# Three edits to the gates of a two-layer decoder kernel: where the decay rates are exponentiated, how the skips are loaded, and how the gates' weights lie

## The chip, the cores and the metric

The kernel runs on one core of a Trainium2 chip. The time is the device time of one execution in microseconds (us). A profile of one further execution is at hand: for every engine, the start and length of each instruction, and what each engine waited for. The engines are PE (TensorE, matrix products), DVE (VectorE), ACT (ScalarE), POOL (GpSimd) and SP (SyncE, which only issues transfers). "PEld" are the weight loads of PE, which run beside its matmuls.

## The reference, cut to what matters

The program is a decoder trunk of two layers on 512 tokens of width 1024. Each layer is a half-step SwiGLU feed-forward, a mixer, and a second half-step feed-forward. Layer 0's mixer is a Mamba-2 head group beside an mLSTM head group; layer 1's is a sparse attention. The change touches the gates of layer 0's mixer and the small parameters that go with them:

```python
z, xbc, dt_raw, qm, km, vm, om, ig, fg = split_cols(h @ w_in, HY_SPLITS)   # dt_raw: 16 columns, ig: 4, fg: 4
dt = softplus(dt_raw + dt_bias)          # (512, 16)
A  = -exp(a_log)                         # the decay rates, 16 numbers
y  = ssd_chunked(xs, dt, A, B, C, 128)
y  = y + xs * d_skip[:, None]            # the skips, 16 numbers, one for each head of 64 channels
hm = mlstm_chunked(qm, km, vm, ig + igate_bias, fg + fgate_bias, 128)
```

Everything is float32. The kernel holds a float32 matrix as two parts, a high part that the matmul's reduced format holds exactly and the low rest, and forms a product from three matmuls: high by high, high by low, low by high.

## The kernel before, in words

The kernel runs six stages in turn: `ffn00`, `mix0` (layer 0's mixer), `ffn01`, `ffn10`, `mix1` and `ffn11`. It keeps the activations in SBUF, channels on partitions, and streams the weights: SP loads a block of a weight matrix into one of four buffers (`raw`), ACT and DVE split it into its two parts in one of five buffers (`form`: ACT copies the high part, L240 or L501, and DVE subtracts it from the raw block, L243 or L503), and PE multiplies.

**The feed-forward stages** take the 2816 hidden columns 256 at a time, in eleven units. From the third unit on, a unit's products are seven half-size products in the manner of Strassen (`seven`, from L626): their weights are sums and differences of four raw blocks (DVE, L496), they accumulate in PSUM pairs `pA`, `pB` and `pD`, and ACT copies some intermediate sums out of PSUM (`keep`, L651) before PE may go on adding to the same pair. Some blocks are split in another way: ACT writes the negated high part (L534), a transfer issued by POOL adds the raw block to it (L535), and ACT writes the high part (L536). One unit is 168 matmuls. The order of the instructions in these stages is set by a planner in the kernel (`Plan`), which gives each step a cost and a due time and issues the steps in the order of its own plan; `plan.tail` holds the last instruction planned for each engine.

**The stage `mix0`** is written out in program order, and a scheduler of the compiler, which works on modelled times, orders it. It may also move instructions of `mix0` ahead into `ffn00` where they depend on nothing there. `hybrid` first weaves `gates` (from L1095) with `conv` (from L1018). `gates` loads the 24 gate columns of the input projection for the eight blocks of 128 channels (L1100 to L1102), loads the small parameters (L1104 to L1110), exponentiates and negates the decay rates (L1112, L1113), splits the gate weights (L1114), and multiplies: 24 matmuls of 24 weight columns by 512 tokens into `pgate` (L1117). The statement `issue_after(self.loads[AMID].ins)` (L1105) holds the small loads behind the 31st weight load of `ffn00`. Then `settle` sums the squares of the activations (`pssq`, L417), raises the mean to the power -1/2 on POOL (L430), and spreads the result over the partitions (`prow`, L438, and ACT, L465); every product of the stage is scaled by it (`rrow`). The gates are scaled (L1121), turned so that tokens lie on partitions (`pgt`, L1124), given their biases (L1133), and taken through a chain of small DVE steps to the decays of both head groups (L1134 to L1204). `conv` is six pairs of projections (`pxbc`), each 24 matmuls of 128 columns by 512 tokens, scaled (`u`, L1028), convolved (L1030 on POOL, L1033 on DVE) and activated (L1037).

The small parameters lie in one 128-column row of the constants, `consts[:, 7]`. Columns 72 to 119 hold the biases (24), the decay rates (16) and the skips (8 for each half of the partitions). Columns 32 to 63 hold the rotary frequencies of layer 1, written by 32 memsets on POOL (L1415).

Of the kernel before, what the change touches and what calls it, by code (L numbers as in the profile page):

```python
# [10 lines left out]
F32 = mybir.dt.float32  # L11
F32R = mybir.dt.float32r
AF = mybir.ActivationFunctionType
ALU = mybir.AluOpType
AX = mybir.AxisListType

P = 128
T = 512
NB = T // P
D = 1024  # L20
KC = D // P
# [193 lines left out]
class Trunk:  # L215
# [879 lines left out]
    def gates(self, w, cols, g):  # L1095


        nc = self.nc
        a = self.a
        raw = self.ring("raw")[1][:, 0 : KC * 24].rearrange("p (n w) -> p n w", w=24)  # L1100
        for o, c, n in cols:
            nc.sync.dma_start(raw[:, :, o : o + n], w[:, c : c + n].rearrange("(k p) n -> p k n", p=P))  # L1102

        vec = self.consts[:, 7, 72:120]  # L1104
        with self.tc.issue_after(self.loads[AMID].ins):  # L1105
            for o, n, name in ((0, 16, "hy_dt_bias"), (16, 4, "hy_fgate_bias"), (20, 4, "hy_igate_bias"), (24, 16, "hy_a_log")):
                nc.sync.dma_start(vec[:, o : o + n], a[name].partition_broadcast(P))
            ds = a["hy_d_skip"].rearrange("e (c two) -> two (e c)", two=2)
            for h in range(2):
                nc.sync.dma_start(vec[h * 64 : (h + 1) * 64, 40:48], ds[h].partition_broadcast(64))  # L1110
        gbias, nega, self.dskip = vec[:, 0:24], vec[:, 24:40], vec[:, 40:48]
        nc.scalar.activation(nega, nega, AF.Exp)  # L1112
        nc.vector.tensor_scalar(nega, nega, -1.0, None, op0=ALU.mult)  # L1113
        f = self.form(raw)  # L1114
        ps = self.mmps("pgate")
        for k in range(KC):
            self.mm3(ps[0:24], (f[0][:, k], f[1][:, k]), (self.xg[0][k], self.xg[1][k]), k == 0, k == KC - 1)  # L1117
        self.settle()
        yield
        t = self.tmp.tile([24, T], F32, name="gt", tag="t1")  # L1120
        nc.vector.tensor_tensor(t, ps[0:24], self.rrow[0:24], op=ALU.mult)  # L1121
        pt = self.aux("pgt", (NB, P))
        for b in range(NB):
            nc.tensor.transpose(pt[:, b, 0:24], t[:, b * P : (b + 1) * P], self.ident[0:24, 0:24])  # L1124
        box, used = self.box, [0]

        def st(name, n):
            used[0] += NB * n
            return box[:, used[0] - NB * n : used[0]].rearrange("p (b n) -> p b n", b=NB)

        tt, ts, stt = nc.vector.tensor_tensor, nc.vector.tensor_scalar, nc.vector.scalar_tensor_tensor
        x = st("gx", 24)
        tt(x, pt[:, :, 0:24], gbias.unsqueeze(1).to_broadcast([P, NB, 24]), op=ALU.add)  # L1133
        ts(x[:, :, 16:20], x[:, :, 16:20], -1.0, None, op0=ALU.mult)  # L1134


# [1 line left out]
        u, s, z, p = st("gu", 20), st("gs", 20), st("gz", 20), st("gp", 20)  # L1138
# [762 lines left out]
```

## Time and profile before

| | us |
|---|---|
| median of 3 runs | 2011.41 |
| lowest, highest | 2008.55, 2012.13 |
| the profiled execution's own time | 2005.02 |
| its span, first to last instruction | 2003.3 |
| PE busy | 1963.0 (98% of the span) |
| DVE busy | 1589.9 (79%) |
| ACT busy | 1172.9 (59%) |
| POOL busy | 272.7 (14%) |
| mean granted TensorE clock | 0.996 of full speed |

In the rows of the profile, "L501" is line 501 of the kernel; "form<-raw" is what an instruction writes and reads, buffer numbers left out. A row of a timeline has the start and the length in us, engine, line, operation, tiles and shapes, how many, and in brackets how long the engine sat idle before it and what ended that. Matmuls overlap, so a matmul's length is more than the distance to the next one. A row of the table of windows has the stretch, its length, the busy time of PE, PEld, DVE, ACT and POOL with the number of instructions, the granted TensorE clock, the mean busy share of the 16 DMA engines and GB/s. A row of transfers ends with the median time from issue to landing. `ACT_TABLE_LOAD` is ACT's change from one set of functions to another; "SPq" is SP's queue of transfers.

### The profile page before, as it was taken

To read this page: it belongs to the slowest core of one execution; us is meant where nothing else is said; L and a number is where in the kernel's file an instruction comes from. 1 tells how busy PE (TensorE), PEld (TensorE's weight loads), DVE (VectorE), ACT (ScalarE), POOL (GpSimd) and SP (SyncE) were. 2 spreads that over 40 slices of the span, in tenths; PEclk is the share of its full clock that TensorE was granted. 3 is DMA by queue.
4 is the path that set the end of the run, shared out by engine and by line. 5 is a ranking of instruction groups with operands and counts; after the bars stand their busy time and mean duration, and the time that the engine had idled before them with its cause. 6 is when DMAs were issued, how large, how long until landed. Compare 5 with 4: busy or idle time off the path is not lost. (4 is left out here: it accounts for less than half of the span.)

```text
span 2003.3 us, 34305 instructions
## 1 busy us (share of the span) xinstructions
PE 1963.0 (98%) x13828; PEld 1782.7 (89%) x13828; DVE 1589.9 (79%) x2348; ACT 1172.9 (59%) x1718; POOL 272.7 (14%) x335
## 2 busy tenths in 40 slices
PE   8999999999999999999999999999999999999998
PEld 6999999787788888999998899999966577999998
DVE  7988878886547648988888998978779948989886
ACT  6756657442345434757566566756668644757564
POOL 1000101321101011001002000101214421101010
PEclk9999999999999999999999999999999999999999
DMA  8565666433331232666665356665754202666564
GB/s 221 138 168 139 148 168 148 129 106 116 103 98 62 77 97 71 165 152 166 154 163 140 103 148 167 159 161 143 181 136 105 64 5 80 155 162 169 147 171 114
DMA packets 214438, 265.47 MB, mean 133 GB/s; under 512 B 14140, under 2 KB 187400, under 8 KB 214280
## 3 DMA queue, kind: packets, MB, share of 16 engines
q1 hardware_dynamic: 193632, 190.87, 32.1%
q0 software_dynamic: 20448, 72.36, 19.4%
q8 instruction: 108, 1.77, 0.4%
q14 instruction: 50, 0.41, 0.1%
q10 hardware_dynamic: 200, 0.06, 0.0%
HBM read 188.77 MB, written 2.14 MB: 95 GB/s over the span
## 5 line engine op out<-in xcount | busy, mean ns | idle before, releaser
L503 DVE TENSOR_TENSOR form<-raw,form 128x1024 fp32r<-128x1024 f32 (+1 forms) x327 | 387.2, 1188 | 106.2 <-ACT form L501 104.5
L501 ACT ACTIVATE form<-raw 128x1024 fp32r<-128x1024 f32 (+1 forms) x327 | 335.2, 1028 | 195.5 <-DVE raw L496 134.7
L281 PE MATMUL pA<-xf,form 128*128 128x256 f32 x1152 | 322.3, 280 | 2.5 <-ACT ft L651 2.4
L283 PE MATMUL pA<-xf,form 128*128 128x256 f32 x1152 | 321.9, 279 | 0.0
L282 PE MATMUL pA<-xf,form 128*128 128x256 f32 x1152 | 321.8, 279 | 0.0
L496 DVE TENSOR_TENSOR raw<-raw 128x1024 f32<-128x1024 f32 (+2 forms) x241 | 283.6, 1180 | 20.8 <-DMA raw<-in_ffn_w_up 9.5
L535 POOL DMA_DIRECT2D form<-raw x136 | 116.9, 860 | 1193.4 <-ACT form L534 1139.0
L281 PEld LDWEIGHTS pA<-xf,form 128*128 128x128 f32 x1152 | 216.9, 188 | 3.1 <-ACT ft L651 2.6
L282 PEld LDWEIGHTS pA<-xf,form 128*128 128x128 f32 x1152 | 216.8, 188 | 0.2
L283 PEld LDWEIGHTS pA<-xf,form 128*128 128x128 f32 x1152 | 216.9, 188 | 0.0
L534 ACT ACTIVATE form<-raw 128x1024 fp32r<-128x1024 f32 (+1 forms) x136 | 140.2, 1032 | 130.0 <-PE pD L283 68.4
L282 PE MATMUL pA<-hid,form 128*128 128x256 f32 x704 | 198.3, 282 | 2.8 <-DVE hid L503 2.8
L281 PE MATMUL pA<-hid,form 128*128 128x256 f32 x704 | 198.9, 283 | 0.5 <-ACT hid L501 0.5
L283 PE MATMUL pA<-hid,form 128*128 128x256 f32 x704 | 197.4, 280 | 0.0
L281 PE MATMUL pD<-xf,form 128*128 128x256 f32 x576 | 160.6, 279 | 0.0
L282 PE MATMUL pD<-xf,form 128*128 128x256 f32 x576 | 160.6, 279 | 0.0
L283 PE MATMUL pD<-xf,form 128*128 128x256 f32 x576 | 160.5, 279 | 0.0
L496 DVE TENSOR_TENSOR ft<-ft 128x256 f32<-128x256 f32 (+2 forms) x288 | 146.9, 539 | 4.4 <-ACT ft L754 0.4
L536 ACT ACTIVATE form<-raw 128x1024 fp32r<-128x1024 f32 (+1 forms) x136 | 139.0, 1023 | 0.0
L282 PEld LDWEIGHTS pA<-hid,form 128*128 128x128 f32 x704 | 132.3, 188 | 4.4 <-DVE hid L503 4.2
L281 PEld LDWEIGHTS pA<-hid,form 128*128 128x128 f32 x704 | 132.5, 188 | 1.4 <-ACT hid L501 0.9
L283 PEld LDWEIGHTS pA<-hid,form 128*128 128x128 f32 x704 | 132.4, 188 | 0.0
(450 smaller groups left out, 5168.0 us busy)
## 6 DMA issues: line engine op xcount, KB each, us to landing
form<-raw POOLq DMA_DIRECT2D x120, 512.0 KB, 5.9
raw<-in_ffn_w_gate SPq DMA_DIRECT2D x88, 512.0 KB, 4.6
raw<-in_ffn_w_up SPq DMA_DIRECT2D x88, 512.0 KB, 4.0
raw<-in_ffn_w_down SPq DMA_DIRECT2D x64, 512.0 KB, 4.9
raw<-in_hy_w_in SPq DMA_DIRECT2D x44, 512.0 KB, 3.8
raw<-in_ffn_w_down SPq DMA_DIRECT2D x32, 384.0 KB, 3.8
raw<-in_hy_w_out SPq DMA_DIRECT2D x16, 512.0 KB, 3.5
form<-raw POOLq DMA_DIRECT2D x16, 384.0 KB, 4.3
```

The lines of the kernel that those rows point to most:

```text
L281: mm(out, l[0], r[0], start=start, stop=False)
L282: mm(out, l[0], r[1], start=False, stop=False)
L283: mm(out, l[1], r[0], start=False, stop=stop)
L496: (self.p if pool else self.v)(n, lambda: e.tensor_tensor(out(), x(), y(), op=op), reads, writes)
L501: self.s(n, lambda: self.highs.append(nc.scalar.activation(hi(), src(), AF.Copy)), srck, hik)
L503: n, lambda: nc.vector.tensor_tensor(lo(), src(), hi().bitcast(F32), op=ALU.subtract), srck + hik, lok
L534: self.s(n, lambda: nc.scalar.activation(f()[:, 1], raw, AF.Copy, scale=-1.0), rawk, lok)
L535: self.plan.add("gpsimd", 0.85, lambda: nc.gpsimd.dma_start(f()[:, 1], raw, accum_op=ALU.add), rawk + lok, lok, 5.5)
L536: self.s(n, lambda: nc.scalar.activation(f()[:, 0], raw, AF.Copy), rawk, hik)
```

## The change

Three edits in `gates`. The exponential and the negation of the decay rates, and the spreading of the skips, are held behind the last planned instruction of ACT and of DVE. The skips are loaded by one transfer of the 16 numbers as they lie in memory, to columns 32 to 47 of the constants' row, and DVE copies the even ones to the eight skip columns of partitions 0 to 63 and the odd ones to those of partitions 64 to 127. The two parts of the gates' weights are laid side by side, 24 high and 24 low columns for each block of 128 channels, so that one matmul of 48 columns makes high by high and low by high, and one of 24 columns makes high by low; the two halves of the result are added after the turn.

```diff
-        vec = self.consts[:, 7, 72:120]
+        vec, skips = self.consts[:, 7, 72:120], self.consts[:, 7, 32:48]
         with self.tc.issue_after(self.loads[AMID].ins):
             for o, n, name in ((0, 16, "hy_dt_bias"), (16, 4, "hy_fgate_bias"), (20, 4, "hy_igate_bias"), (24, 16, "hy_a_log")):
                 nc.sync.dma_start(vec[:, o : o + n], a[name].partition_broadcast(P))
-            ds = a["hy_d_skip"].rearrange("e (c two) -> two (e c)", two=2)
-            for h in range(2):
-                nc.sync.dma_start(vec[h * 64 : (h + 1) * 64, 40:48], ds[h].partition_broadcast(64))
+            nc.sync.dma_start(skips, a["hy_d_skip"].partition_broadcast(P))
         gbias, nega, self.dskip = vec[:, 0:24], vec[:, 24:40], vec[:, 40:48]
-        nc.scalar.activation(nega, nega, AF.Exp)
-        nc.vector.tensor_scalar(nega, nega, -1.0, None, op0=ALU.mult)
-        f = self.form(raw)
+        for h in range(2):
+            half = slice(h * 64, h * 64 + 64)
+            with self.tc.issue_after(self.plan.tail[mybir.EngineType.DVE]):
+                nc.vector.tensor_copy(self.dskip[half], skips[half].rearrange("p (c two) -> p two c", two=2)[:, h])
+        with self.tc.issue_after(self.plan.tail[mybir.EngineType.Activation]):
+            nc.scalar.activation(nega, nega, AF.Exp)
+            nc.vector.tensor_scalar(nega, nega, -1.0, None, op0=ALU.mult)
+        f = self.ring("any")[1][:, 0, 0 : KC * 48].rearrange("p (k i n) -> p k i n", i=2, n=24)
+        self.split(f[:, :, 0], f[:, :, 1], raw)
         ps = self.mmps("pgate")
         for k in range(KC):
-            self.mm3(ps[0:24], (f[0][:, k], f[1][:, k]), (self.xg[0][k], self.xg[1][k]), k == 0, k == KC - 1)
+            products = [
+                lambda start, stop: nc.tensor.matmul(
+                    ps[0:48], f[:, k].rearrange("p i n -> p (i n)"), self.xg[0][k], start=start, stop=stop
+                ),
+                lambda start, stop: nc.tensor.matmul(ps[0:24], f[:, k, 0], self.xg[1][k], start=start, stop=stop),
+            ]
+            if k == KC - 1:
+                products.reverse()
+            for i, product in enumerate(products):
+                product(k == 0 and i == 0, k == KC - 1 and i == 1)
...
-        t = self.tmp.tile([24, T], F32, name="gt", tag="t1")
-        nc.vector.tensor_tensor(t, ps[0:24], self.rrow[0:24], op=ALU.mult)
+        t = self.tmp.tile([48, T], F32, name="gt", tag="t1")
+        nc.vector.tensor_tensor(t, ps[0:48], self.rrow[0:48], op=ALU.mult)
...
-            nc.tensor.transpose(pt[:, b, 0:24], t[:, b * P : (b + 1) * P], self.ident[0:24, 0:24])
+            nc.tensor.transpose(pt[:, b, 0:48], t[:, b * P : (b + 1) * P], self.ident[0:48, 0:48])
...
-        tt(x, pt[:, :, 0:24], gbias.unsqueeze(1).to_broadcast([P, NB, 24]), op=ALU.add)
+        tt(x, pt[:, :, 24:48], gbias.unsqueeze(1).to_broadcast([P, NB, 24]), op=ALU.add)
+        tt(x, x, pt[:, :, 0:24], op=ALU.add)
```

## The prediction

> **What bounds the kernel now.** The busy times of the whole span (PE 98%) say little of one stage, so I read the table of windows by stage first.
>
> ```profile
> 120.00:340.00 220.00, 216.43 (x1814) 215.62 (x1814) 179.98 (x222) 136.60 (x177) 18.88 (x22) 0.99 0.62 153
> 340.00:620.00 280.00, 280.00 (x1465) 224.53 (x1463) 189.70 (x310) 120.82 (x178) 50.68 (x39) 1.00 0.38 110
> ```
>
> The first stretch is most of `ffn00`, the second the part of `mix0` that the change touches. PE has no gap at all in the second and 3.6 us of gaps in the first. Both are bound by PE, so an edit there is worth what it takes out of PE's queue, and an edit on another engine is worth nothing unless PE was waiting for it. The next view is therefore PE's own waits from 100 to 200 us, and then the timelines around the longest.
>
> ```profile
> PE pA L281 <- ACT ft L651: 2.4, 1, 2.4
> ```
> ```profile
> 147.24 0.28 PE L281 MATMUL pB<-xf,form 128*128 128x256 f32 x1
> ...
> 149.95 0.28 PE L283 MATMUL pB<-xf,form 128*128 128x256 f32 x1
> 152.60 0.39 PE L281 MATMUL pA<-xf,form 128*128 128x256 f32 x1 [2.37 <-ACT ft L651]
> ...
> 157.07 0.28 PE L281 MATMUL pD<-xf,form 128*128 128x256 f32 x1
> ```
> ```profile
> 146.18 1.28 ACT L1112 ACT_TABLE_LOAD   x1
> 151.84 0.22 ACT L1112 ACTIVATE raw<-raw 128x16 f32<-128x16 f32 x1 [4.38 <-DMA raw<-in_hy_a_log]
> 151.97 0.58 ACT L651 ACTIVATE ft<-pA 128x512 f32<-128x512 f32 x1
> ```
>
> The scheduler has moved the exponential (L1112) out of `mix0` into a feed-forward unit. ACT reaches it at 146.2, and a queue in order stands there until the rates have been loaded: 4.38 us. Behind it stands the copy L651, which PE needs before it may add to `pA` again. The product of 24 matmuls that starts at 152.60 would have started one step after 149.95.
>
> ```profile
> 152.00:154.00 2.00, 1.40 (x9) 1.40 (x10) 0.65 (x2) 1.49 (x3) 0.00 (x0) 0.84 0.09 1
> 154.00:156.00 2.00, 2.00 (x11) 2.00 (x11) 1.97 (x3) 0.00 (x0) 0.00 (x0) 0.50 0.05 0
> ```
>
> After the gap PE runs at half its clock for a while (granted clock 0.84 in the mean of the first two us, 0.50 in the next).
>
> **The change part by part.**
>
> *The exponential, off the unit.* The 24 matmuls of `pB` start from 147.24 to 149.95, 23 steps of 0.118 us. The next product would run from 149.95 + 0.12 = 150.07 for 24 x 0.118 = 2.83 us, and the one after it (`pD`) would start at 152.90 and not at 157.07: **4.17 us** off PE, of which 2.53 us are the wait and 1.64 us the slow clock.
>
> What is late next, when PE is 4.17 us earlier? Its next inputs are the copy L651 itself, ready 0.6 us after its sums, and weights that come through SP's queue, where the skips stand.
>
> ```profile
> raw<-in_hy_d_skip SPq DMA_DIRECT2D x2, 2.0 KB, 9.7
> ...
> raw<-in_hy_dt_bias SPq DMA_DIRECT2D x1, 8.0 KB, 7.5
> ```
> ```profile
> 150.88 0.39 SPq L514 DMA_DIRECT2D raw<-in_ffn_w_up  x1
> ```
> ```profile
> 161.20 1.23 DVE L496 TENSOR_TENSOR raw<-raw 128x1024 f32<-128x1024 f32 x1 [2.11 <-DMA raw<-in_ffn_w_up]
> ...
> 164.07 1.22 DVE L503 TENSOR_TENSOR form<-raw,form 128x1024 fp32r<-128x1024 f32 x1
> ```
> ```profile
> 165.55 0.28 PE L281 MATMUL pD<-xf,form 128*128 128x256 f32 x1
> ```
>
> *The skips as they lie.* 2 KB in two transfers take 9.7 us to land, and the windows above show why it matters: from 152 to 156 the DMA engines are at 5 to 9% and move nothing, while a 512 KB block issued at 150.88 waits behind them and lands only at 161.2. Today that is harmless: the form made from it is ready at 165.3 (164.07 + 1.22), and the product that uses it (the one after the `pD` product of 165.55, 24 x 0.118 later) starts at 168.4. With PE 4.17 us earlier that product is due at 164.2, so without the new load PE would stall about 1 us there. The new load has 128 runs of 64 bytes like `a_log`'s, where the old two had 1024 runs of 4 bytes. I expect it to land like `dt_bias` (7.5 us, behind the same blocks), and the block after it some 6 us sooner. So this edit's own worth on PE is nothing, but it covers the first: 1 us if it fails.
>
> *The gates' matmuls.* 24 become 16, all 512 columns long.
>
> ```profile
> 350.89 0.39 PE L281 MATMUL pgate<-xgn,form 128*24 128x512 f32 x1
> ...
> 352.51 0.28 PE L281 MATMUL pA<-hid,form 128*128 128x256 f32 x1
> ```
>
> Seven take 352.51 - 350.89 = 1.62 us, 0.231 each, as long as the full-width `pxbc` ones: the rows stream at one pace however many weight columns there are, so 48 columns cost what 24 do. 8 x 0.231 = **1.85 us** off a PE that has no gap.
>
> *What is added, off PE.* The exponential, with its table load, now stands on ACT behind the last square of `mix0`'s start, and a second load brings the set of Silu back.
>
> ```profile
> 362.88 1.05 ACT L240 ACTIVATE form<-raw 128x1024 fp32r<-128x1024 f32 x1
> 367.77 1.06 ACT L240 ACTIVATE form<-raw 128x1024 fp32r<-128x1024 f32 x1 [3.85 <-PE pgate L282]
> ...
> 380.85 0.63 ACT L1037 ACTIVATE bc<-acc 128x512 f32<-128x512 f32 x1 [0.58 <-DVE acc L1033]
> ```
> ```profile
> 364.77 1.41 DVE L496 TENSOR_TENSOR ssq<-ssq 128x512 f32<-128x512 f32 x2
> ```
> ```profile
> 367.80 0.95 PE L417 MATMUL pssq<-raw,ssq 128*128 128x1 f32 x8
> ...
> 374.44 0.60 PE L438 MATMUL prow<-raw 128*128 128x128 f32 x4
> ```
>
> 1.28 + 0.22 = 1.5 us ahead of the form of 362.88, and ACT has 3.85 us free behind it. In the order in which the built program's instructions stand that form's DVE part now stands ahead of the last addition of squares, for which `pssq` waits: form done at 365.4 (362.88 + 1.5 + 1.05), its rest 1.2 us later at 366.7, the addition (half of 1.41) at 367.4. `pssq` itself comes three matmuls later in the new order (67 of 512 columns ahead of it, not 64), at 368.5. The cover is 1.1 us. The second load stands ahead of the first Silu, which has 0.58 us free before it; the 0.7 us left over delay an output that PE reads only after the convolutions. Both loads I put at nothing. [...]
>
> ```profile
> 416.94 1.28 ACT L1169 ACT_TABLE_LOAD   x1
> 418.24 0.26 ACT L1169 ACTIVATE raw<-raw 128x64 f32<-128x64 f32 x1
> ```
>
> DVE gains one more addition on the turned gates and two copies of 64x8.
>
> ```profile
> 383.74 0.25 DVE L1133 TENSOR_TENSOR raw<-pgt,raw 128x96 f32<-128x96 f32 x1
> ...
> 412.05 0.17 DVE L1155 TENSOR_SCALAR raw<-raw 128x16 f32<-128x16 f32 x1
> ...
> 421.68 0.69 DVE L1028 TENSOR_TENSOR u<-pxbc,raw 128x512 f32<-128x512 f32 x1 [0.30 <-PE pxbc L283]
> ```
> ```profile
> 415.52 0.34 PE L1158 MATMUL pcs<-raw 128*128 128x80 f32 x2
> ```
>
> The addition costs at most 0.25. The copies have no row; the nearest small op is L1155, so 0.1 to 0.25 each. What needs them is the gates' chain, which ends for PE at `pcs`: ready at 412.2, wanted at 415.5, 3.3 us of cover. In the new order `pcs` comes five matmuls (1.15 us) earlier, which leaves about 2 us.
>
> *What the diff does not say.* The skips now lie where layer 1's frequencies are written later. In the built order the 32 memsets (L1415), first on POOL until now, stand between the last sum of squares and the power L430, behind DVE's two copies.
>
> ```profile
> L1415 POOL MEMSET raw<- x32: 99/99/100, 1.8 to 2.9; 128x1 f32 x32
> ```
> ```profile
> 369.03 1.97 POOL L430 TENSOR_TENSOR raw<-raw 128x4 f32<-128x4 f32 x1 [6.72 <-DVE raw L429]
> ```
>
> Queued behind them is the power, and PE waits for it in `prow`. At their own pace they take 1.1 us (1.8 to 2.9); bounded by POOL's other tiny op, 1.97 each, 63 us. I take 1.1, the same instruction and shape. They would run from about 367.6 to 368.8; the power could start 1.2 us after `pssq` (369.03 - 367.80), at 369.7, or a form later, ends near 372, and PE reaches `prow` at about 374.2 (88 long matmuls after the first gate, not 89). Cost on the path nothing; POOL has 374.2 - 1.97 - 367.6 = 4.6 us for the memsets before PE waits.
>
> **The sum**: -4.17 - 1.85 = **-6.0 us**. The profiled execution would go from 2005.02 to 1999.0; the median of the runs, 6.4 us above it, from 2011.41 to **2005.4**.
>
> **The rivals.**
>
> *R1, the slow stretch stays* (or another comes). If the half clock after 153 is not the gap's doing, 1.64 us come back: -4.4, 2007.0. The trace speaks against it: two like stretches elsewhere also follow a broken PE.
>
> ```profile
> 1096.00:1098.00 2.00, 0.57 (x4) 0.22 (x3) 1.90 (x4) 0.49 (x1) 0.00 (x0) 1.00 0.83 198
> 1098.00:1100.00 2.00, 2.00 (x12) 1.71 (x12) 2.00 (x5) 0.00 (x0) 0.86 (x1) 0.71 0.94 324
> ...
> 1550.00:1552.00 2.00, 1.23 (x5) 0.30 (x3) 1.93 (x7) 2.00 (x5) 0.64 (x2) 1.00 0.00 0
> ...
> 1668.00:1670.00 2.00, 2.00 (x10) 1.73 (x11) 0.94 (x3) 0.00 (x0) 0.98 (x1) 0.72 0.00 0
> ```
>
> But at 1550 the clock held, so it also depends on how a gap falls, and shifting all later work by 6 us can add or take away such a stretch: 1.6 us either way in the range. [...] Chance 0.12.
>
> *R2, DVE becomes the bound in the convolution*, and PE's 1.85 us end in waits: -4.2, 2007.2. For it: DVE has work without a break from the first scaled product on, and it starts at `prow`, which moves only 0.2 us. Against it: at 421.68 DVE was waiting for PE, and PE has several banks and forms in hand. Chance 0.10. R1 and R2 together (-2.5, 2008.9) have 0.05.
>
> *R3, slower: the memsets in front of the power.* [...] Beyond 0.14 us each PE stalls at `prow` and then runs slow for 1.6 us; from about 0.3 us each (32 x 0.3 = 9.6, less 4.6, plus 1.6 is 6.6) the change loses. At 0.5 us each it is 16.0 - 4.6 + 1.6 - 6.0 = +7.0, 2018.4. Nothing shows a memset that slow. Chance 0.10.
>
> *R4, it doesn't do what it says*: the skips' transfer stays slow, and PE stalls 1 us at the product named above: -5.0, 2006.4, chance 0.05; it lies within the forecast's range.
>
> **How the numbers follow.** The forecast has 0.58 (0.63 with R4). What a measurement of this kernel can tell from no change is about 0.2%, 4.0 us, a time under 2007.4. The runs before lie from 2.9 below to 0.7 above their median. Low end: 2005.4 less 2.9 and less 1.6 for a slow stretch gone elsewhere, 2001.0. High end: R1 with R2, 2008.9, plus 0.7 and 1.6, 2011.2. That leaves out R3 (0.10) and the rarer mishaps of the rest. Faster: nine in ten of 0.63, 0.57, and a little over half of R1 and R2, 0.12, together 0.69. Same: the rest of these and both at once, 0.21. Slower: R3, 0.10.
>
> **What would show it.** Right: no ACT wait for `a_log` near 146 to 152, PE without a gap from 138 to 200 at clock 1.00, `pD` one product after `pB`; the `w_up` block landing some 4 us after its issue; 16 `pgate` rows and an unbroken PE through 340 to 620; memsets of 1.1 us ending before the power is due. Wrong: a gap in PE at `prow`, `pssq` or `pcs`, a product after 160 that waits for a transfer, or a granted clock below 1 in `ffn00`.

## The result and the profile after

The changed kernel takes 2005.23 us (median of 17 runs, 1998.71 to 2009.17), the kernel before 2010.34 in as many runs of the same occasions. The ratio is 0.9967, with an interval of 0.9953 to 0.9980: 6.6 us faster, 4.0 to 9.4. (The medians of all runs differ by 5.1; the ratio is taken from the fast runs alone.) The forecast was 6.0.

The profiled execution seems to say the opposite: its span is 2005.1 us, where that of before was 2003.3. So the span has to be cut into the part where the change acts and the part where it doesn't. Marks that both kernels have are the transfers that POOL issues (L535). Four of them, first in before, then in the changed kernel (start, length):

```profile
93.17 0.86 POOL L535 DMA_DIRECT2D form<-raw  x1 [9.03 <-ACT form L534]
...
268.35 0.86 POOL L535 DMA_DIRECT2D form<-raw  x1 [5.30 <-ACT form L534]
...
797.01 0.92 POOL L535 DMA_DIRECT2D form<-raw  x1 [34.32 <-ACT form L534]
...
1985.40 0.86 POOL L535 DMA_DIRECT2D form<-raw  x1 [7.21 <-ACT form L534]
```
```profile
94.79 0.85 POOL L535 DMA_DIRECT2D form<-raw  x1 [9.38 <-ACT form L534]
...
265.08 0.86 POOL L535 DMA_DIRECT2D form<-raw  x1 [5.30 <-ACT form L534]
...
792.04 0.92 POOL L535 DMA_DIRECT2D form<-raw  x1 [34.32 <-DMA raw<-in_ffn_w_gate]
...
1987.20 0.85 POOL L535 DMA_DIRECT2D form<-raw  x1 [7.21 <-ACT form L534]
```

From the first mark to the second lies the unit with the exponential: 175.18 us before, 170.29 after, **4.89 gained**. From the second to the third lies `mix0`: 528.66 and 526.96, **1.70 gained**. The rest, which no edit touches, took 1188.39 and 1195.16, **6.77 lost**, and the start lost 1.62 before any edit acts. Nearly all of the loss in the rest is one event. Windows of the changed kernel (PE busy is the first number after the length, the clock the third from the end):

```profile
952.00:954.00 2.00, 0.81 (x7) 0.60 (x6) 1.69 (x2) 0.35 (x1) 0.00 (x0) 1.00 0.00 0
954.00:956.00 2.00, 0.38 (x1) 0.19 (x1) 1.97 (x4) 1.81 (x4) 0.00 (x0) 0.98 0.55 175
956.00:958.00 2.00, 1.34 (x6) 1.35 (x7) 1.93 (x5) 2.00 (x4) 0.64 (x1) 0.50 0.25 87
...
962.00:964.00 2.00, 2.00 (x16) 2.00 (x16) 1.45 (x2) 0.11 (x1) 0.00 (x0) 0.81 0.62 146
```
```profile
952.31 1.23 DVE L496 TENSOR_TENSOR raw<-raw 128x1024 f32<-128x1024 f32 x1 [3.98 <-DMA raw<-in_ffn_w_down]
```

A block of `w_down` came late, PE stood idle for 3.5 us and then ran at half clock to 963. Whether that belongs to the change is a question for the experiments. The places that the prediction named look as it wanted them. Windows of the changed kernel for `ffn00` and `mix0`, then the timeline of the unit:

```profile
120.00:336.00 216.00, 215.26 (x1822) 214.85 (x1821) 180.94 (x222) 134.72 (x176) 18.84 (x22) 1.00 0.62 156
336.00:614.00 278.00, 278.00 (x1458) 223.97 (x1456) 189.31 (x314) 122.67 (x179) 50.86 (x71) 1.00 0.36 111
```
```profile
149.07 0.60 ACT L651 ACTIVATE ft<-pA 128x512 f32<-128x512 f32 x1 [1.28 <-PE pA L283]
...
151.58 0.28 PE L283 MATMUL pB<-xf,form 128*128 128x256 f32 x1
151.70 0.28 PE L281 MATMUL pA<-xf,form 128*128 128x256 f32 x1
...
154.01 0.38 SPq L514 DMA_DIRECT2D raw<-in_ffn_w_up  x1
...
157.47 1.22 DVE L496 TENSOR_TENSOR raw<-raw 128x1024 f32<-128x1024 f32 x1 [0.92 <-DMA raw<-in_ffn_w_up]
```

PE's idle time in `ffn00` fell from 3.6 to 0.7 us at a clock of 1.00, and in `mix0` it has none. The copy L651 runs long before PE needs it, `pA` follows `pB` at the usual step (0.12 us), and the block behind the skips lands 3.5 us after its issue (10.3 before).

### The profile page after: what moved, and what is told of

The parts are those of the page before. It is cut to its first block, busy times and chain, and to the rows that moved or that the text cites. A ratio compares the mean times of both kernels' runs of the same rounds, so it can differ in the third digit from the quotient of the medians.

```text
span 2005.1 us, 34288 instructions
## 1 busy us (share of the span) xinstructions
PE 1965.8 (98%) x13820; PEld 1785.3 (89%) x13820; DVE 1589.9 (79%) x2351; ACT 1172.3 (58%) x1718; POOL 271.3 (14%) x335
## 5 line engine op out<-in xcount | busy, mean ns | idle before, releaser
L496 DVE TENSOR_TENSOR raw<-raw 128x1024 f32<-128x1024 f32 (+2 forms) x241 | 283.6, 1181 | 21.1 <-DMA raw<-in_ffn_w_down 11.3
L535 POOL DMA_DIRECT2D form<-raw x136 | 116.7, 858 | 1195.5 <-ACT form L534 1106.5
L496 DVE TENSOR_TENSOR ft<-ft 128x256 f32<-128x256 f32 (+2 forms) x288 | 146.9, 540 | 4.4 <-ACT ft L754 0.4
```

What stands on the lines that cost most here:

```text
L496: (self.p if pool else self.v)(n, lambda: e.tensor_tensor(out(), x(), y(), op=op), reads, writes)
L535: self.plan.add("gpsimd", 0.85, lambda: nc.gpsimd.dma_start(f()[:, 1], raw, accum_op=ALU.add), rawk + lok, lok, 5.5)
```

## The experiments

First the changed kernel was run again, beside each of its three edits alone.

**The changed kernel again.**

> The changed kernel once more, for a second profile on another occasion. In the first one PE gained 4.2 us at 152 and 1.7 us in mix0, and lost 6.6 us at 952 to 965, where a w_down block came late: a gap of about 3 us and then 7 us at half clock. Theory A (the late block is the luck of one execution): time 6 us below before, no half clock at 950 to 965 in this profile, span about 1999. Theory B (the work after mix0 now meets the transfers in another phase, so the block is late every time): the same gap and slow stretch at about 952 again, span about 2005, and the median cannot be 6 us below before.

Measured: 0.9971 (0.9957 to 0.9985), -5.8 us. No slow stretch at 952 (PE busy 3.87 of the 4 us from 952), and the span is 2000.4. Theory A holds: the late block doesn't come in every execution of the changed kernel. Of the 14 profiles of this document one more has it, that of the skips alone below, where PE stood idle for 3.3 us near 962. What makes it late stays open.

**The exponential alone**

```diff
-        nc.scalar.activation(nega, nega, AF.Exp)
-        nc.vector.tensor_scalar(nega, nega, -1.0, None, op0=ALU.mult)
+        with self.tc.issue_after(self.plan.tail[mybir.EngineType.Activation]):
+            nc.scalar.activation(nega, nega, AF.Exp)
+            nc.vector.tensor_scalar(nega, nega, -1.0, None, op0=ALU.mult)
```

> Only the exponential and the negation are moved; the skips are loaded in two transfers of 4-byte runs as before, the gates stay 24 matmuls. Forecast's theory: the ACT wait and the slow clock at 152 go (-4.2), but the w_up block behind the skips still lands some 10 us after its issue, and a product after 160 waits about 1 us for it: -3.2 in all, clock 1.00 from 138 to 160. Rival 1 (the half clock at 153 is not the gap's doing): -2.5 and a stretch of clock 0.50 near 150. Rival 2 (the slow skips harm nobody): -4.2 and no wait of PE between 150 and 200.

Measured: 0.9998 (0.9982 to 1.0013), -0.4 us, -3.6 to +2.6. The clock is 1.00 from 144 to 176, so rival 1 falls; the stall is where it was foretold, so rival 2 falls too. Its timeline:

```profile
154.81 0.38 SPq L514 DMA_DIRECT2D raw<-in_ffn_w_up  x1
...
163.39 1.23 DVE L496 TENSOR_TENSOR raw<-raw 128x1024 f32<-128x1024 f32 x1 [5.70 <-DMA raw<-in_ffn_w_up]
...
165.36 0.36 PE L281 MATMUL pD<-xf,form 128*128 128x256 f32 x1 [1.05 <-DVE ft L496]
```

The block takes 8.6 us behind the two transfers of 4-byte runs, and PE waits 1.05 us for what is made of it, then 0.6 us for a form near 178.

**The skips alone**

```diff
-            ds = a["hy_d_skip"].rearrange("e (c two) -> two (e c)", two=2)
-            for h in range(2):
-                nc.sync.dma_start(vec[h * 64 : (h + 1) * 64, 40:48], ds[h].partition_broadcast(64))
+            nc.sync.dma_start(skips, a["hy_d_skip"].partition_broadcast(P))
...
+                nc.vector.tensor_copy(self.dskip[half], skips[half].rearrange("p (c two) -> p two c", two=2)[:, h])
```

> Only the skips' load is changed (one transfer of 64-byte runs and two DVE copies; the 32 memsets move in front of the power); the exponential stays in the feed-forward unit. Forecast's theory: nothing (0), because PE still waits 2.4 us for ACT behind the rates and only the block after the skips lands sooner; the memsets cost nothing. Rival 1 (the 1024 runs of 4 bytes also delay the rates, which share the queue): the rates land sooner, the wait of 4.4 us shrinks, and up to -4.2. Rival 2 (memsets in front of the power cost): above 0, with a gap at prow.

Measured: 1.0006 (0.9991 to 1.0022): nothing, as forecast. PE has no wait from 336 to 616, so rival 2 falls. Rival 1 falls as well, for the rates came no sooner: ACT waited 5.67 us for them here, 4.38 in before. The windows show PE's wait, 3.66 us, and a longer slow stretch:

```profile
152.00:154.00 2.00, 0.00 (x0) 0.00 (x0) 0.00 (x0) 0.00 (x0) 0.00 (x0) 1.00 0.22 29
154.00:156.00 2.00, 0.34 (x1) 0.35 (x2) 0.17 (x1) 1.10 (x3) 0.00 (x0) 0.51 0.18 28
156.00:158.00 2.00, 2.00 (x11) 2.00 (x11) 1.39 (x2) 0.55 (x1) 0.00 (x0) 0.50 0.68 237
...
160.00:162.00 2.00, 2.00 (x16) 2.00 (x15) 0.88 (x2) 1.97 (x3) 0.00 (x0) 0.78 0.00 0
```

**The gates alone**

```diff
-            self.mm3(ps[0:24], (f[0][:, k], f[1][:, k]), (self.xg[0][k], self.xg[1][k]), k == 0, k == KC - 1)
+                    ps[0:48], f[:, k].rearrange("p i n -> p (i n)"), self.xg[0][k], start=start, stop=stop
...
+        tt(x, x, pt[:, :, 0:24], op=ALU.add)
```

> Only the gates' weights are laid side by side (16 matmuls in place of 24, one more DVE addition); the exponential and the skips stay. Forecast's theory: 8 x 0.231 = -1.85, PE without a gap from 340 to 620 and the gap at 150 still there. Rival (DVE becomes the bound in the convolution): 0, and PE waits between 380 and 430.

Measured: 0.9996 (0.9983 to 1.0010), -0.8 us with -3.4 to +2.0: -1.85 is inside, and so is nothing. In this execution the wait at 151 was short (1.85 us), and no slow clock followed right behind it (one came at 227, behind another wait of 1.85 us):

```profile
150.00:152.00 2.00, 1.02 (x9) 0.81 (x7) 0.00 (x0) 0.00 (x0) 0.00 (x0) 1.00 0.64 93
152.00:154.00 2.00, 1.14 (x9) 1.14 (x10) 0.38 (x2) 1.65 (x3) 0.00 (x0) 1.00 0.06 1
154.00:156.00 2.00, 2.00 (x19) 2.00 (x18) 1.97 (x2) 0.00 (x0) 0.00 (x0) 1.00 0.04 0
```

The three edits alone add up to nothing, and together they give 6 us. Either that is scatter, or two of them need each other. The next three kernels leave one edit out of the change each.

**Without the gates' edit** (against the changed kernel)

```diff
-                    ps[0:48], f[:, k].rearrange("p i n -> p (i n)"), self.xg[0][k], start=start, stop=stop
...
+            self.mm3(ps[0:24], (f[0][:, k], f[1][:, k]), (self.xg[0][k], self.xg[1][k]), k == 0, k == KC - 1)
```

> The exponential moved and the skips in one transfer; the gates stay 24 matmuls. Theory (the two edits work only together, because either alone leaves PE waiting at 150 or at 164): -4.2 to -5 against before, no PE wait between 140 and 200, w_up landing 4 us after its issue. Rival (each edit is worth what it was alone, -0.4 and +1.2, so nothing): about 0.

Measured: 0.9976 (0.9960 to 0.9991), -4.8 us. No wait of PE from 130 to 200; `w_up` is issued at 152.53 and at work by 156.09.

**Without the skips' edit** (against the changed kernel)

```diff
-            nc.sync.dma_start(skips, a["hy_d_skip"].partition_broadcast(P))
+            ds = a["hy_d_skip"].rearrange("e (c two) -> two (e c)", two=2)
+            for h in range(2):
+                nc.sync.dma_start(vec[h * 64 : (h + 1) * 64, 40:48], ds[h].partition_broadcast(64))
...
-                nc.vector.tensor_copy(self.dskip[half], skips[half].rearrange("p (c two) -> p two c", two=2)[:, h])
```

> The changed kernel with the skips in two transfers of 4-byte runs again (no DVE copies, memsets first on POOL again). Theory: the changed kernel's -6 less the stall behind the late w_up block, which the profile of the exponential alone has at 1.05 us (164) and some 0.6 us after it: -4.5, with a wait of PE near 162 to 165 and clock 1.00 through 150. Rival 1 (the skips' load is worth nothing): -6. Rival 2 (moving the memsets cost time): below -6.

Measured: 0.9968 (0.9956 to 0.9980), -6.4 us, where -4.5 was expected; both are inside. The stall is there (1.1 us, PE for DVE L496, at 164), and the clock is 1.00. By time alone rival 1 can't be told from the theory; the segments below tell them apart.

**Without the exponential's edit** (against the changed kernel)

```diff
-        with self.tc.issue_after(self.plan.tail[mybir.EngineType.Activation]):
-            nc.scalar.activation(nega, nega, AF.Exp)
+        nc.scalar.activation(nega, nega, AF.Exp)
```

> The changed kernel with the exponential where it was, in the feed-forward unit. Theory: only the gates' -1.85 is left, PE waits 1.8 to 3.7 us at 150 for ACT, and runs at half clock for none, one or two stretches of 3.4 us behind it, as the gap falls into one or two of them. Rival (the skips' load already frees the rates): -5 to -6 and no wait at 150.

Measured: 0.9991 (0.9979 to 1.0004), -1.8 us. PE waits 1.9 us at 151 and runs one stretch at half clock, as in before.

**The exponential back in the unit, its rates earlier**

```diff
-        with self.tc.issue_after(self.plan.tail[mybir.EngineType.Activation]):
+        with self.tc.issue_after(self.loads[AMID - 2].ins):
+            nc.sync.dma_start(vec[:, 24:40], a["hy_a_log"].partition_broadcast(P))
...
+        with self.tc.issue_after(self.highs[57].ins):
             nc.scalar.activation(nega, nega, AF.Exp)
```

> The changed kernel, but with the exponential back at its old place on ACT (behind the split ahead of the copy L651) and the rates loaded two weight blocks earlier. Theory (the wait for the rates is the cost, not the exponential's place): ACT's load of 1.28 and exponential of 0.22 run from about 146 to 147.7, ahead of the copy due at 150, so -6 like the changed kernel and no PE wait at 150. Rival (ACT's 1.5 us and the second table load in a unit are the cost): PE waits for ACT near 150 or 158, -3 or less.

Measured: 0.9974 (0.9960 to 0.9989), -5.2 us. It is the wait, not the place: on ACT the load and the exponential stand where they stood, with the rates at hand, and the copy behind them is in time.

```profile
147.64 1.28 ACT L1118 ACT_TABLE_LOAD   x1
148.94 0.21 ACT L1118 ACTIVATE raw<-raw 128x16 f32<-128x16 f32 x1
149.06 0.58 ACT L651 ACTIVATE ft<-pA 128x512 f32<-128x512 f32 x1
```

**All of them by segment.** The same four marks as above, in us, from one profile of each kernel (the ratios come from all its runs); the rest is what the edits don't touch. "Unit" means the exponential in the feed-forward unit.

| exponential | skips | gates | with the unit | mix0 | rest | ratio |
|---|---|---|---|---|---|---|
| unit (before) | two loads | 24 | 175.2 | 528.7 | 1188.4 | 1 |
| unit | one | 24 | 177.9 | 528.7 | 1197.4 | 1.0006 |
| unit | two | 16 | 176.8 | 527.0 | 1190.7 | 0.9996 |
| unit | one | 16 | 175.1 | 527.0 | 1190.1 | 0.9991 |
| moved | two | 24 | 174.1 | 528.7 | 1190.3 | 0.9998 |
| moved | two | 16 | 171.9 | 527.0 | 1190.9 | 0.9968 |
| moved | one | 24 | 170.2 | 528.7 | 1187.8 | 0.9976 |
| moved (changed, 3 profiles) | one | 16 | 170.3, 170.1, 170.5 | 527.0, 526.9, 526.9 | 1195.2, 1192.0, 1188.9 | 0.9967, 0.9971, 0.9961 |
| unit, rates early | one | 16 | 170.0 | 526.9 | 1189.8 | 0.9974 |

Read it by columns. `mix0` takes 528.65 to 528.66 with 24 matmuls and 526.90 to 527.00 with 16: the gates' edit is worth 1.7 us, each time. The first column is 175.1 to 177.9 with the wait, 171.9 and 174.1 with the wait gone but the skips slow, 170.0 to 170.5 with both gone. So the exponential and the skips do need each other: alone, the exponential gains 1.1 us in its own segment (175.2 to 174.1), for the late block takes back most of the 4.2, and the skips gain nothing while PE waits for the rates. The gates' 1.7 is there alone too, but it is less than the 3 us or so to which one ratio is known, because the rest scatters over 9.6 us from one execution to the next. With four pairs of ratios for each edit (kernels that differ in it alone; of the changed kernel the mean of its three ratios) the exponential is worth 0.4, 6.0, 5.6 and 5.0 us, mean 4.3; the gates 0.8, 6.0, 3.0 and 2.0, mean 3.0; the skips -1.2, 4.4, 1.0 and 0.4, mean 1.2. From the ratios' intervals each of these means is good to about 2 us.

**Useless work in the wait.** To see whether idleness causes the half clock, PE was given something to do in before's wait:

```diff
+    def idle_work(self, n):
+        junk = self.aux("junk", (P,))
+        for _ in range(n):
+            self.nc.tensor.matmul(junk, self.ident, self.ident, start=True, stop=True)
...
+        self.products = getattr(self, "products", 0) + 1
+        if self.products == 321:
+            self.idle_work(20)
```

> The kernel before, with 20 useless products of 128x128 by 128x128 (into a spare PSUM tile that nothing reads) in PE's queue right ahead of the product that waits for ACT at 150. The useless work takes about 2.4 us, the length of the wait; ACT's wait for the rates stays. Theory (the half clock is the doing of PE's idleness): no clock of 0.50 from 148 to 162, an idle PE of less than 1.5 us there, and on average some 1.5 us less than before (the four profiles with this wait so far lost 1.6, 0, 2.6 and 1.6 us to the slow clock), up to the useless work's own surplus where the wait is short. Rival R1 (the slow stretch has another cause): clock 0.50 for 3.4 us at about 153 as before, time at or above before.

Measured: 0.9991 (0.9974 to 1.0009), -1.8 us. ACT's wait was there, longer than in before, and the clock stayed (ACT's L659 is L651 of before):

```profile
151.01 4.62 PE L281 MATMUL junk<-raw 128*128 128x128 f32 x40
...
153.56 0.21 ACT L1120 ACTIVATE raw<-raw 128x16 f32<-128x16 f32 x1 [5.16 <-DMA raw<-in_hy_a_log]
153.68 0.58 ACT L659 ACTIVATE ft<-pA 128x512 f32<-128x512 f32 x1
...
155.40 0.36 PE L289 MATMUL pA<-xf,form 128*128 128x256 f32 x1
```
```profile
152.00:154.00 2.00, 2.00 (x20) 2.00 (x19) 0.18 (x1) 0.44 (x2) 0.00 (x0) 1.00 0.07 1
154.00:156.00 2.00, 2.00 (x20) 2.00 (x19) 0.76 (x1) 1.21 (x2) 0.00 (x0) 1.00 0.05 0
```

The time says nothing either way. The clock speaks against R1, but this is one execution: without the useless work PE would have stood idle from 151.01 to about 154.26, and the gates alone had such a wait (1.85 us) with no half clock behind it either. The runs below fill four more waits and settle it. One useless product is in the record twice and takes 0.22 us on PE ((155.40 - 151.01) / 20), not 0.12: the 20 ran 1.1 us past the end of the copy (153.68 + 0.58).

**Useless work in four other waits of the changed kernel** (a key counts the kernel's products up to the wait, a negative one stands ahead of the `pssq` that follows that product; the value says how many useless products go there)

```diff
+FILL = {2241: 10, -2242: 10, 3109: 26, -3374: 22}
```

> The changed kernel with useless products (same as in the run before this one) ahead of four waits that its profiles show at 1097, 1099, 1433 and 1670: 10, 10, 26 and 22 of them, a little shorter than each wait. The ten profiles so far lost about 2.2, 3.0 and 1.8 us to the slow clock behind these waits. Theory (idleness causes it, and PE bounds what follows): those stretches run at clock 1.00, and the time is some 5 to 7 us below the changed kernel, 11 to 13 below before. Rival (what follows those waits is not bound by PE, or the useless work delays the product behind it): the clock is 1.00 but the time stays at the changed kernel's -6.

Measured: 0.9950 (0.9932 to 0.9968), -10.0 us; beside it the changed kernel had -7.8. The slow stretches behind the four waits are gone, but by the ratios only some 2 us with them, where 5 to 7 were expected; with such wide intervals the timeline has to say why. The size of the useless work was wrong, as its timeline shows; the `pssq` that had waited 2.9 us now starts 4.9 us after the useless work did, 2.0 later than it need:

```profile
1662.87 5.07 PE L282 MATMUL junk<-raw 128*128 128x128 f32 x44
1667.78 0.95 PE L427 MATMUL pssq<-raw,ssq 128*128 128x1 f32 x8
```

**The changed kernel a third time, beside the two**

> The changed kernel a third time, beside the two runs above on one chip: -6 against before (0.997). Profile: no wait of PE from 138 to 200, and, if the late block at 952 was the luck of one execution, no half clock there.

Measured: 0.9961 (0.9947 to 0.9975), -7.8 us; span 2000.8, no wait of PE from 138 to 200 and no half clock at 952 (PE was idle for 0.2 us there).

**Half as much useless work**

```diff
-FILL = {2241: 10, -2242: 10, 3109: 26, -3374: 22}
+FILL = {2241: 6, -2242: 5, 3109: 13, -3374: 11}
```

> The changed kernel with useless products ahead of the same four waits, but 6, 5, 13 and 11 of them: the run with 10, 10, 26 and 22 showed that one takes 0.22 us on PE, not the 0.12 assumed, so that they ran 1 to 2.5 us past each wait's end and gave back what the clock had gained. At 0.22 they take 1.3, 1.1, 2.9 and 2.4 us, within waits of 1.5, 1.4, 3.4 and 2.9. Theory: clock 1.00 behind these waits and 6 to 7 us below the changed kernel, 12 to 14 below before (ratio about 0.9935). Rival (what follows those waits isn't bound by PE): like the changed kernel, 0.9965.

Measured: **0.9935** (0.9916 to 0.9954), 1996.16 us (6 runs), -13.1 us: 5 to 7 below the changed kernel's three results, as expected, with some 4 us of uncertainty. The three places in the changed kernel's third profile, then here:

```profile
1080.00:1110.00 30.00, 26.46 (x125) 20.88 (x125) 27.37 (x33) 16.38 (x26) 8.14 (x6) 0.94 0.36 109
1415.00:1440.00 25.00, 21.61 (x155) 21.50 (x154) 23.13 (x29) 19.31 (x33) 9.93 (x9) 0.86 0.70 190
1655.00:1680.00 25.00, 22.11 (x114) 18.67 (x114) 16.57 (x25) 12.18 (x19) 4.42 (x3) 0.93 0.24 72
```
```profile
1080.00:1110.00 30.00, 28.87 (x148) 23.62 (x149) 29.03 (x34) 16.92 (x24) 6.76 (x5) 1.00 0.40 122
1415.00:1440.00 25.00, 24.41 (x199) 24.30 (x198) 20.56 (x27) 19.30 (x31) 11.67 (x11) 1.00 0.70 186
1655.00:1680.00 25.00, 24.46 (x130) 20.66 (x129) 20.72 (x29) 15.24 (x22) 3.15 (x3) 1.00 0.28 85
```

The clock there was 0.86 to 0.94 and is 1.00. This is what decides against R1: in each of the 12 profiles without useless work in these waits the clock fell to 0.50 near 1100, 1430 and 1670, in the two with it at none of the three. By the marks used above the rest took 1182.3 us here, against 1188.9 to 1195.2 in the changed kernel's three profiles. This is the fastest of all kernels here, by doing more work.

## Why the prediction was right, point by point

- **The exponential, -4.17.** Right in mechanism, and a little small. It was sized from one execution, and the wait varies: PE's idle time plus what the half clock cost (busy time by one less the clock, in windows of 2 us) came to 2.4 + 1.6, 1.8 + 0, 3.7 + 2.6 and 1.9 + 1.6 us in the four profiles with the wait, 3.9 in the mean. The segment that holds it, with all that follows from it, fell from 176.3 (mean of four) to 170.2, by 6, when the wait and the slow skips were both gone; by time this edit is worth 4.3, give or take 2.
- **What is late next, and the skips.** Right: "the product that uses it" waited 1.05 and 1.1 us in the two profiles with the old skips, against the 1 us worked out, and not at all with the new load. "It covers the first" was right too, but "1 us if it fails" was too little: the cover is worth 1.7 us in one pair of segments (171.9 to 170.2) and 3.9 in the other (174.1 to 170.2), since later waits follow the first (at 168, 178 and 225 in the profile of the exponential alone). The new transfer itself lands hardly sooner, 8.5 us after its issue (`dt_bias` 8.2); what changed is the block behind it, 3.5 us for 10.3. One reading was off without consequence: the two old transfers hold 2 KB each, 4 in all.
- **The gates, -1.85.** The term was 0.15 too large: 1.70 in each pair. The pace of 0.231 us held with 48 columns (347.62 to 347.85). The gates' own matmuls gave what was forecast: from start to start the 24 took 5.58 us in before and the 16 take 3.74 to 3.77 in the changed kernel's three profiles, 1.81 to 1.84 less. Of this, 0.10 to 0.13 come back in the 288 `pxbc` matmuls, which run among them (66.56 us before, 66.66 to 66.69 after); why these take longer stays open.
- **Edits costed at nothing.** All held: PE has no wait from 336 to 614 in any of the three profiles of the changed kernel. There, the memsets took 1.29 us (1.1 worked out), ended before DVE had the power's input ready, and so R3 falls:

```profile
364.15 1.29 POOL L1431 MEMSET raw<- 128x1 f32 x32 [5.14 <-DVE raw L1114]
366.64 1.04 POOL L430 TENSOR_TENSOR raw<-raw 128x4 f32<-128x4 f32 x1 [1.20 <-DVE raw L429]
```

The load starts 0.02 us behind the instruction ahead of it (359.05 + 0.63), the exponential 0.01 us behind the load (359.70 + 1.28), so here the load took ACT its own 1.28 us and no more:

```profile
359.05 0.63 ACT L816 ACTIVATE ssq<-raw 128x512 f32<-128x512 f32 x1 [0.76 <-POOL ssq L496]
359.70 1.28 ACT L1116 ACT_TABLE_LOAD   x1
360.99 0.22 ACT L1116 ACTIVATE raw<-raw 128x16 f32<-128x16 f32 x1
```

- **R1** fell by experiment: with four waits filled, the clock held at 1.00 behind all of them. **R2** fell: `mix0` kept its 1.7 us in every pair. **R4** fell: the block behind the skips came early. Its 1 us was the first stall alone (1.05 and 1.1); with the waits that follow the price is the 1.7 to 3.9 above.
- **The scatter.** "1.6 us either way" for slow stretches elsewhere was too narrow for one execution: the rest of the program varied by 9.6 us. It averages out over the runs. That the changed kernel's median, 2005.23, lies 0.2 from the forecast of 2005.4 is in part luck: the median of before, from which the forecast was counted, was 2011.41 in 3 runs and 2010.34 in 17, and the gain itself is known to 2.7 us.

## What to carry to other kernels

The wait on the bounding engine cost its length (1.8 to 3.7 us in four profiles) and then what the half clock behind it cost (0 to 2.6 us), and both differed from one execution to the next, so size such a term from several profiles. Two edits on one chain can each be worth nothing alone: after removing a wait, ask which transfer is late next, and test pairs. Where a wait on PE can't be removed, try useless products that fit inside it: here they kept the clock at 1.00 where it had been 0.86 to 0.94. But measure one of them first, for work that outlasted its wait (by 2.0 us at one `pssq`) came to -10.0 us where half as much came to -13.1.

## What the runs showed of the hardware

**The clock changes on a grid.** In all 14 profiles the clock fell to 0.50 somewhere (in the last kernel's only at 14.8 and at 1991, its start and its end), and within one execution all falls lie whole multiples of 3.413 us apart, with another offset in each execution. The first and the last fall in before, in windows of 0.1 us:

```profile
153.30:153.40 0.10, 0.10 (x3) 0.10 (x2) 0.00 (x0) 0.10 (x1) 0.00 (x0) 0.74 0.06 0
...
1668.80:1668.90 0.10, 0.10 (x2) 0.08 (x1) 0.10 (x2) 0.00 (x0) 0.00 (x0) 0.83 0.00 0
```

By the mean clock of each window they are at 153.35 and 1668.87, 444 steps of 3.4133; the two falls between them, read in the same way, are at 1098.84 and 1429.94, 277 and 374 such steps behind the first. Up to the last few us of an execution a half-clock stretch lasts one or two such steps, so by the clock of 0.50 it costs a PE that is busy throughout half of that, an estimated 1.7 or 3.4 us. The executions were cut along this grid, from 100 us on and without the last kernel's. Behind a window at full clock with more than 1.87 us of idle PE the next one always ran at half clock (29 of 29), behind 1.09 to 1.87 us sometimes (28 of 79), behind less never (0 of 7026). Behind a window at half clock another one followed in 19 of 76 cases, after as little as no idle time at all. What decides in the middle stays open; two windows in a row of before, with 1.57 and 1.43 us idle, show that it isn't the sum alone:

```profile
1092.01:1095.43 3.42, 1.85 (x8) 1.22 (x8) 3.42 (x4) 1.87 (x4) 0.83 (x1) 1.00 0.15 51
1095.43:1098.84 3.41, 1.98 (x13) 1.49 (x13) 3.31 (x5) 1.06 (x2) 0.00 (x0) 1.00 0.73 200
1098.84:1102.25 3.41, 3.41 (x9) 2.64 (x10) 2.68 (x5) 0.00 (x0) 1.48 (x1) 0.50 0.31 110
```

The grid also accounts for the wait of 1.8 us in the profile of the gates alone, behind which the clock held: there a step ended at 151.9, in the middle of the wait, and the halves of 0.90 and 0.95 us were both below the 1.09 us under which no window at full clock was followed by a half clock.

**The pace of the same matmuls differs.** In nine of the 14 profiles the 256-column matmuls run 4% faster for about 70 us near the end (in a tenth for some 10 us), with PE never idle and the clock at 1.00. Before, then the exponential alone:

```profile
1800.00:1840.00 40.00, 40.00 (x355) 40.00 (x354) 36.40 (x46) 27.31 (x38) 3.43 (x4) 1.00 0.66 170
```
```profile
1800.00:1840.00 40.00, 40.00 (x342) 40.00 (x341) 35.07 (x45) 26.59 (x36) 3.43 (x4) 1.00 0.63 163
```

355 matmuls in 40 us against 342. By these numbers (4% of 70 us) it is worth some 3 us, and it is part of the scatter in the rest; no view here shows its cause.
